# Feed-forward weight sums of an encoder trunk: from GpSimd to VectorE and to accumulating loads

## The chip, the cores and the metric

The kernel runs on one core of a Trainium2 chip. The core has five engines with a queue of instructions each: TensorE (PE: matrix products into PSUM banks), VectorE (DVE), ScalarE (ACT), GpSimd (POOL) and SyncE (SP, which here only issues loads and stores). An engine takes its instructions in order; one that waits for a semaphore holds up all behind it. Sixteen DMA engines move data between device memory and SBUF. The metric is device time of one execution in microseconds, lower is better.

## The reference

The reference is an encoder trunk for 512 tokens of width 1024: two layers, each with a feed-forward, a token mixer, an attention into 256 memory tokens and a second feed-forward. Each ends in a layer norm. All is float32.

```python
def swiglu(x, w_gate, w_up, w_down):
    return (jax.nn.silu(x @ w_gate) * (x @ w_up)) @ w_down
...
    for i in range(DEPTH):
        y = swiglu(x, ffn_w_gate[i, 0], ffn_w_up[i, 0], ffn_w_down[i, 0])
        x = layer_norm(ALPHA * x + 0.5 * y, ln_g[i, 0], ln_b[i, 0])
        ...
        y = swiglu(x, ffn_w_gate[i, 1], ffn_w_up[i, 1], ffn_w_down[i, 1])
        x = layer_norm(ALPHA * x + 0.5 * y, ln_g[i, 3], ln_b[i, 3])
```

The change touches the four calls of `swiglu` alone. Their hidden width is 2816.

## The kernel before

**Precision.** TensorE is fed with the rounded type float32r. To keep float32 accuracy each operand is split: ScalarE copies it rounded (the high part), VectorE subtracts that from the original (the low part). `split` does both, `wide` does it for a block of weights into two new buffers. Each product is then three matmuls (`mm3`): high by high, high by low, low by high.

**Groups.** `ffn` cuts the hidden width into five groups of 512 columns and a rest. Of the first group most is done apart; for the other four the gate and the up projection (1024 x 512 weights each) are multiplied by a 2 x 2 block scheme with seven products in place of eight. Such a projection is called a half-chunk in what follows; it is one call of `quarters`. Its weights are four quarters of 512 x 256: a (upper rows, first columns c1), b (lower rows, c1), c (upper, c2), d (lower, c2). The products, by the scheme's numbers and in the order of the program, need these weights: 1: a; 6: a + c + d; 5: c + d; 2: b; 7: a + c; 4: d; 3: a + b + c + d. The tokens' sums are made once per feed-forward. The way down (512 rows of `w_down`) is done the same way by `down_steps`, with quarters "11", "12", "21", "22" of 256 x 512, and the sums t1 = 12 + 11 (product 5), t2 = t1 + 22 (product 6), t2 + 21 (product 4) and 12 + 22 (product 7).

**Steps.** Each product is a step with three parts: `load` (issues the loads of its weights), `prep` (sums, splits) and `product` (matmuls, and what reads the bank after them). `pipeline` writes the parts in an order in which a step's load stands three steps ahead of its product and its prep two. A group is 14 products of the gate and up half-chunks (24 matmuls of 256 columns each), each paired with one of 14 pieces of the previous group's way down (6 matmuls of 512 columns each).

**Who adds.** `mix(..., aside)` puts a sum on GpSimd where `aside` is true, else on VectorE. On GpSimd are, per half-chunk, v = a + c (into a new buffer) and c = c + d (in place); per way down t1 = 12 + 11 (new buffer) and 12 = 12 + 22 (in place): 32 x 2 + 20 x 2 = 104 sums of 128 x 1024 elements. On VectorE are a = a + c and a = a + b, and t2 = t1 + 22 and t2 = t2 + 21.

**What sets the order.** Nothing runs when the methods are called. `Recorder` stores every instruction as an `Op` with its operands; `Graph.emit` then plans them: it steps through time with an assumed cost per instruction (`Graph.cost`) and an assumed delay until its result can be used, and each engine takes the ready instruction that was recorded first. The order in which the plan starts instructions is the order on the engines' queues. Since all of them are issued from `emit` and `record`, the profile gives nearly all of them one line, L143, and they are told apart by the names of their tiles. Loads by SyncE are assumed to be usable 2000 ns after their issue cost, DMAs issued by GpSimd 4000 ns after 700 ns.

**Buffers.** Weights, sums, split parts and hidden activations all lie in `slab` buffers of 128 x 1024 float32, of which there are 27 (`BUFS`). They are given out in the order of the calls of `slab`; a load waits until the buffer that it is given is free. In PSUM there are three banks "a" (hidden products), two "d" and three "t" (down products and others).

The only accumulating loads before are in `add_x`: GpSimd issues four DMAs of 128 rows of 4 KB that add x onto what stands in SBUF (`accum_op=ALU.add`), in the first feed-forward.

## Time and profile before

| | |
|---|---|
| median of 3 runs | 2236.86 us (2235.01 to 2237.48) |
| profiled execution | 2237.42 us, span 2235.6 us |
| TensorE busy | 2153.6 us (96%), granted clock 0.992 |
| VectorE busy | 1821.6 us (81%) |
| ScalarE busy | 1060.4 us (47%) |
| GpSimd busy | 556.4 us (25%), of it 295.1 us in the 104 weight sums, 2838 ns each on average |
| device memory | 219.27 MB read, 100 GB/s over the span |

The span runs from the first to the last instruction of the profiled execution; the rest of its time lies around it. Busy times are sums over the whole span. Since stages differ, the prediction reads stretches of the span and not these shares. "a<-raw,slab" in a row means: writes a bank "a", reads tiles "raw" and "slab". A product of a hidden group shows as MATMUL into "a", its way down as MATMUL into "d" and "t". In the chain's rows "x24" counts matmuls, and 24 of them make one product. PE's busy time has modelled ends.

### The profile page before, as it was taken

Reading aid. Unit: us, or ns where it says so; the run is one execution under the profiler, and the core shown is the slowest. Engines: PE = TensorE matmul, PEld = TensorE weight load, DVE = VectorE, ACT = ScalarE, POOL = GpSimd, SP = SyncE. Lnnn points to the kernel's source line nnn. Section 1 sums busy time; section 2 is a strip of 40 time slices with the busy share of each in tenths; the row PEclk is TensorE's granted clock in tenths of the full one; section 3 lists DMA queues with packets and bytes.
Section 4 is the critical chain, followed back from the end, with each engine's and each line's share of the span. In section 5 each row is a group of like instructions: output and inputs, shape, how many; then the busy total and the mean of one; then the engine's idle time right before and its main releaser. Section 6 shows DMA issues by size and latency. Waiting matters only on the chain.

```text
span 2235.6 us, 33852 instructions
## 1 busy us (share of the span) xinstructions
PE 2153.6 (96%) x13408; PEld 1924.2 (86%) x13408; DVE 1821.6 (81%) x2429; ACT 1060.4 (47%) x1671; POOL 556.4 (25%) x499
## 2 busy tenths in 40 slices
PE   9999999999999999999999999999999999999997
PEld 7988887778998898888799888888989988988886
DVE  7899998788755869999878999977677558699997
ACT  4554443467443544444534454435554435444442
POOL 2222314544000112232212123314330001122322
PEclk9999999999999999999999999999999999999999
DMA  5432342102432324324323233435554323233241
GB/s 179 136 96 90 109 140 84 38 10 73 133 125 86 112 67 151 95 86 141 95 76 104 86 96 93 156 105 147 154 157 130 115 97 102 67 113 104 87 132 57
DMA packets 182799, 236.15 MB, mean 106 GB/s; under 512 B 9328, under 2 KB 142064, under 8 KB 182640
## 3 DMA queue, kind: packets, MB, share of 16 engines
q1 hardware_dynamic: 178704, 221.14, 32.2%
q0 software_dynamic: 3648, 12.59, 1.9%
q8 instruction: 105, 1.72, 0.3%
q14 instruction: 54, 0.44, 0.1%
q10 hardware_dynamic: 288, 0.26, 0.0%
HBM read 219.27 MB, written 4.19 MB: 100 GB/s over the span
## 4 chain that ended last, share of the span: by engine, by line
PE 67%; DVE 25%; issue 3%; ACT 2%; POOL 1%; DMA 0%; DVEq 0%; SPq 0%; POOLq 0%; ACTq 0%
PE a L143 41%; DVE slab L143 19%; PE d L143 17%; PE t L143 10%; DVE t L143 3%; DVE x L143 2%; ACT slab L143 1%; POOL slab L143 1%; DVE a L143 0%; POOL rms8y L143 0%; ACT t L143 0%; DMA gain<-ab_k_gain 0%; ACT junk L143 0%; POOL lny L143 0%; DMA raw<-x_t 0%
## 5 line engine op out<-in xcount | busy, mean ns | idle before, releaser
L143 DVE TENSOR_TENSOR slab<-slab,slab 128x1024 fp32r<-128x1024 f32 (+3 forms) x582 | 756.3, 1336 | 23.1 <-ACT slab L143 22.3
L143 ACT CAST slab<-slab 128x1024 fp32r<-128x1024 f32 (+2 forms) x478 | 455.5, 984 | 295.3 <-DVE slab L143 150.6
L143 PE MATMUL a<-slab,slab 128*128 128x256 f32 (+3 forms) x2744 | 589.2, 307 | 2.2 <-ACT t L143 1.1
L143 PE MATMUL a<-xh,slab 128*128 128x256 f32 (+2 forms) x2480 | 560.4, 315 | 3.0 <-DVE slab L143 1.9
L143 POOL TENSOR_TENSOR slab<-slab,slab 128x1024 f32<-128x1024 f32 x104 | 295.1, 2838 | 883.2 <-PE t L143 345.8
L143 PEld LDWEIGHTS a<-slab,slab 128*128 128x128 f32 x2744 | 448.0, 191 | 34.2 <-DVE slab L143 5.0
L143 PE MATMUL d<-slab,slab 128*128 128x512 f32 (+2 forms) x1856 | 459.7, 384 | 4.7 <-ACT slab L143 2.9
L143 PEld LDWEIGHTS a<-xh,slab 128*128 128x128 f32 x2480 | 416.8, 191 | 37.4 <-DVE slab L143 2.8
L143 PE MATMUL a<-raw,slab 128*128 128x256 f32 x2048 | 398.2, 287 | 38.7 <-DVE t L143 17.5
L143 PE MATMUL a<-xl,slab 128*128 128x256 f32 (+1 forms) x1240 | 390.5, 315 | 0.0
L143 PEld LDWEIGHTS d<-slab,slab 128*128 128x128 f32 x1856 | 329.7, 190 | 63.9 <-DVE slab L143 4.8
L143 PEld LDWEIGHTS a<-raw,slab 128*128 128x128 f32 x2048 | 331.2, 193 | 59.1 <-DVE slab L143 21.2
L143 PEld LDWEIGHTS a<-xl,slab 128*128 128x128 f32 x1240 | 236.3, 191 | 17.9
L143 PE MATMUL t<-slab,slab 128*128 128x512 f32 (+1 forms) x792 | 195.6, 383 | 1.4 <-DVE x L143 0.7
L143 DVE TENSOR_TENSOR slab<-raw,slab 128x1024 fp32r<-128x1024 f32 (+2 forms) x140 | 172.0, 1248 | 15.8 <-ACT slab L143 15.3
L143 POOL TENSOR_TENSOR t<-t,l 128x256 f32<-128x256 f32 (+2 forms) x104 | 84.6, 835 | 367.9 <-DVE l L143 367.7
L143 PEld LDWEIGHTS t<-slab,slab 128*128 128x128 f32 x792 | 136.6, 189 | 24.1 <-issue 2.4
L143 ACT CAST slab<-t 128x512 fp32r<-128x512 f32 (+2 forms) x205 | 110.1, 563 | 90.0 <-PE t L143 67.5
L143 DVE TENSOR_TENSOR slab<-t,slab 128x512 fp32r<-128x512 f32 (+2 forms) x205 | 126.9, 642 | 17.3 <-ACT slab L143 16.5
L143 ACT CAST slab<-raw 128x1024 fp32r<-128x1024 f32 (+1 forms) x132 | 131.3, 1025 | 18.0 <-DMA raw<-mem_w_kv 7.6
L143 DVE SCALAR_TENSOR_TENSOR x<-d,x 128x512 f32<-128x512 f32 x164 | 111.9, 684 | 34.1 <-PE d L143 33.5
L143 ACT COPY t<-a 128x512 f32<-128x512 f32 x96 | 56.1, 585 | 131.9 <-DVE a L143 97.7
(122 smaller groups left out, 2209.3 us busy)
## 6 DMA issues: line engine op xcount, KB each, us to landing
slab<-ffn_w_gate SPq DMA_DIRECT2D x86, 512.0 KB
slab<-ffn_w_up SPq DMA_DIRECT2D x86, 512.0 KB
slab<-ffn_w_down SPq DMA_DIRECT2D x80, 512.0 KB
slab<-t SPq DMA_DIRECT2D x96, 128.0 KB
raw<-mem_w_kv SPq DMA_DIRECT2D x8, 1024.0 KB
raw<-mem_w_kv SPq DMA_DIRECT2D x16, 512.0 KB
raw<-mem_w_q SPq DMA_DIRECT2D x8, 1024.0 KB
raw<-mem_w_o SPq DMA_DIRECT2D x8, 1024.0 KB
```

The lines of the kernel that those rows point to most:

```text
L143: op.call = lambda: fn(*args, **kw)
```

## The change

No weight sum of the feed-forward is left on GpSimd. In a half-chunk VectorE makes three sums when product 6 is prepared: v = a + c, u = c + d (in c's buffer), a = a + u. After a has been split for product 6, a load adds b onto it from device memory (`plus`), and the result is split again for product 3. b is also loaded plainly, as before, for product 2. In a way down VectorE makes t1 and t2; a load adds "22" onto "12" once t1 is made, and a load adds "21" onto t2 once t2 has been split for product 6. That makes 32 + 40 = 72 accumulating loads of 512 KB, issued by GpSimd, of 512 rows of 1 KB (gate, up) or 256 rows of 2 KB (down). "d" is fetched in the step of product 6 and "12" in that of product 1; the new buffers of v and t1 are taken in `prep` and not in `load`. The planner is told that an accumulating load costs 1200 ns to issue and is usable 9000 ns later.

```diff
@@ class Op, Graph.cost, Graph.record, Graph.emit
-            return max(n * out.ap[0][1] * 4 / 205.0, 600.0) if engine == "sync" else 700.0
+            return max(n * out.ap[0][1] * 4 / 205.0, 600.0) if engine == "sync" else 1200.0 if "accum_op" in kw else 700.0
...
-            end = now[e] + {"sync": 2000.0, "tensor": 160.0}.get(e, 4000.0 if op.dma else 70.0)
+            end = now[e] + {"sync": 2000.0, "tensor": 160.0}.get(e, 9000.0 if op.adds else 4000.0 if op.dma else 70.0)
@@ class Kernel
-    def mix(self, dst, x, y, op, aside=False):
-        (self.nc.gpsimd if aside else self.nc.vector).tensor_tensor(out=dst, in0=x, in1=y, op=op)
+    def plus(self, z, w, q, c):
+        self.nc.gpsimd.dma_start(out=z, in_=w[512 * q : 512 * q + 512, c : c + 256].rearrange("(k p) f -> p k f", p=P), accum_op=ALU.add)
+        return z
+
+    def mix(self, dst, x, y, op):
+        self.nc.vector.tensor_tensor(out=dst, in0=x, in1=y, op=op)
         return dst
@@ quarters
-        places = {1: ("a", 0, c1), 6: ("c", 0, c2), 5: ("d", 1, c2), 2: ("b", 1, c1)}
-
         def load(m):
-            if m in places:
-                name, q, c = places[m]
-                raw[name] = self.quarter(w, q, c)
-            if m == 6:
-                raw["v"] = mix(self.slab(F32, (P, 4, 256)), raw["a"], raw["c"], ALU.add, True)
-            elif m == 5:
-                mix(raw["c"], raw["c"], raw["d"], ALU.add, True)
+            if m == 1:
+                raw["a"] = self.quarter(w, 0, c1)
+            elif m == 6:
+                raw["c"] = self.quarter(w, 0, c2)
+                raw["d"] = self.quarter(w, 1, c2)
+            elif m == 2:
+                raw["b"] = self.quarter(w, 1, c1)
 
         def prep(m):
             if m == 6:
-                mix(raw["a"], raw["a"], raw["c"], ALU.add)
-            elif m == 3:
-                mix(raw["a"], raw["a"], raw["b"], ALU.add)
-            left[m] = self.wide(raw[{1: "a", 6: "a", 5: "c", 2: "b", 7: "v", 4: "d", 3: "a"}[m]])
+                raw["v"] = mix(self.slab(F32, (P, 4, 256)), raw["a"], raw["c"], ALU.add)
+                raw["u"] = mix(raw["c"], raw["c"], raw["d"], ALU.add)
+                mix(raw["a"], raw["a"], raw["u"], ALU.add)
+            left[m] = self.wide(raw[{1: "a", 6: "a", 5: "u", 2: "b", 7: "v", 4: "d", 3: "a"}[m]])
+            if m == 6:
+                self.plus(raw["a"], w, 1, c1)
@@ down_steps
+        def plus(z, name):
+            nc.gpsimd.dma_start(out=z, in_=part(name).rearrange("(b p) f -> p b f", p=P), accum_op=ALU.add)
+
         def load(m):
             if m == 1:
                 fetch("11")
+                fetch("12")
             elif m == 6:
-                fetch("12")
                 fetch("22")
-                raw["t1"] = mix(self.slab(F32, (P, 2, 512)), raw["12"], raw["11"], ALU.add, True)
             elif m == 2:
                 fetch("21")
-                mix(raw["12"], raw["12"], raw["22"], ALU.add, True)
 
         def prep(m):
             if m == 6:
+                raw["t1"] = mix(self.slab(F32, (P, 2, 512)), raw["12"], raw["11"], ALU.add)
                 raw["t2"] = mix(self.slab(F32, (P, 2, 512)), raw["t1"], raw["22"], ALU.add)
+                plus(raw["12"], "22")
...
-            elif m == 2:
-                mix(raw["t2"], raw["t2"], raw["21"], ALU.add)
...
             right[m] = self.wide(raw[{1: "11", 6: "t2", 2: "21", 5: "t1", 3: "22", 7: "12", 4: "t2"}[m]])
+            if m == 6:
+                plus(raw["t2"], "21")
```

**First pair: GpSimd's queue** in the third feed-forward, an up half-chunk, a gate half-chunk, a way down and the next up half-chunk. Before (slab_2212, 2255 and 2303 are "a" of the three half-chunks, slab_2278 is "12"):

```order
L143 TENSOR_TENSOR slab_2216_2297<-slab_2212_2293,slab_2215_2296 128x1024
L143 TENSOR_TENSOR slab_2215_2296<-slab_2215_2296,slab_2225_2306 128x1024
L143 TENSOR_TENSOR slab_2260_2341<-slab_2255_2336,slab_2259_2340 128x1024
L143 TENSOR_TENSOR slab_2259_2340<-slab_2259_2340,slab_2264_2345 128x1024
L143 TENSOR_TENSOR slab_2280_2361<-slab_2278_2359,slab_2261_2342 128x1024
L143 TENSOR_TENSOR slab_2278_2359<-slab_2278_2359,slab_2279_2360 128x1024
L143 TENSOR_TENSOR slab_2307_2388<-slab_2303_2384,slab_2306_2387 128x1024
L143 TENSOR_TENSOR slab_2306_2387<-slab_2306_2387,slab_2316_2397 128x1024
```

Of the changed kernel at the same place (slab_2262 is "12", slab_2285 is t2):

```order
L143 DMA slab_2212_2293<-ffn_w_up 128x4x256
L143 DMA slab_2255_2336<-ffn_w_gate 128x4x256
L143 DMA slab_2262_2343<-ffn_w_down 128x2x512
L143 DMA slab_2285_2366<-ffn_w_down 128x2x512
L143 DMA slab_2303_2384<-ffn_w_up 128x4x256
```

Eight additions have become five issues of accumulating loads, one a half-chunk and two a way down.

**Second pair: VectorE's queue at product 6 of that gate half-chunk.** In it slab_2255 is a, slab_2259 is c; a row that writes x2 or x3 reads a down bank, one that reads "a_" reads a bank of a hidden product. Before:

```order
L143 TENSOR_SCALAR x2_6_87<-d_2251_2332,x2_6_87 128x512
L143 TENSOR_TENSOR slab_2255_2336<-slab_2255_2336,slab_2259_2340 128x1024
L143 TENSOR_SCALAR x3_7_88<-d_2254_2335,x3_7_88 128x512
L143 TENSOR_TENSOR slab_2266_2347<-slab_2255_2336,slab_2265_2346 128x1024
L143 TENSOR_TENSOR slab_2276_2357<-slab_2259_2340,slab_2275_2356 128x1024
```

Of the changed kernel (slab_2265 is v, slab_2260 is d):

```order
L143 TENSOR_TENSOR slab_2265_2346<-slab_2255_2336,slab_2259_2340 128x1024
L143 TENSOR_TENSOR slab_2242_2323<-a_2229_2310,t2_2211_2292 128x512
L143 TENSOR_TENSOR slab_2259_2340<-slab_2259_2340,slab_2260_2341 128x1024
L143 TENSOR_SCALAR x3_7_88<-d_2254_2335,x3_7_88 128x512
L143 TENSOR_TENSOR slab_2255_2336<-slab_2255_2336,slab_2259_2340 128x1024
L143 TENSOR_TENSOR slab_2272_2353<-slab_2261_2342,slab_2271_2352 128x1024
L143 TENSOR_TENSOR t2_2223_2304<-a_2238_2319,t2_2223_2304 128x512
L143 TENSOR_TENSOR slab_2267_2348<-slab_2255_2336,slab_2266_2347 128x1024
```

One sum ahead of the split of product 6 (the row that writes slab_2266, now slab_2267) has become three, with bank reads and another split between them.

**Third pair: VectorE's queue in the first feed-forward's first group, up half-chunk, from the split of product 6 to that of product 3.** Its "a" is slab_107, its "b" slab_125. Before:

```order
L143 TENSOR_TENSOR slab_122_203<-slab_107_188,slab_121_202 128x1024
L143 TENSOR_TENSOR slab_132_213<-t2_129_210,slab_132_213 128x512
L143 TENSOR_TENSOR slab_135_216<-slab_125_206,slab_134_215 128x1024
L143 TENSOR_TENSOR slab_107_188<-slab_107_188,slab_125_206 128x1024
L143 TENSOR_TENSOR a_124_205<-a_124_205,t2_118_199 128x512
L143 TENSOR_TENSOR slab_139_220<-slab_111_192,slab_138_219 128x1024
L143 TENSOR_TENSOR slab_142_223<-slab_82_163,slab_141_222 128x1024
L143 TENSOR_TENSOR slab_143_224<-t2_140_221,slab_143_224 128x512
L143 TENSOR_TENSOR slab_145_226<-slab_120_201,slab_144_225 128x1024
L143 TENSOR_TENSOR slab_148_229<-slab_107_188,slab_147_228 128x1024
```

Of the changed kernel:

```order
L143 TENSOR_TENSOR slab_122_203<-slab_107_188,slab_121_202 128x1024
L143 TENSOR_TENSOR slab_127_208<-slab_110_191,slab_126_207 128x1024
L143 TENSOR_TENSOR slab_131_212<-slab_83_164,slab_130_211 128x1024
L143 TENSOR_TENSOR slab_132_213<-t2_129_210,slab_132_213 128x512
L143 TENSOR_TENSOR slab_135_216<-slab_125_206,slab_134_215 128x1024
L143 TENSOR_TENSOR slab_139_220<-slab_120_201,slab_138_219 128x1024
L143 TENSOR_TENSOR a_124_205<-a_124_205,t2_118_199 128x512
L143 TENSOR_TENSOR slab_142_223<-slab_65_146,slab_141_222 128x1024
L143 TENSOR_TENSOR slab_143_224<-t2_140_221,slab_143_224 128x512
L143 TENSOR_TENSOR slab_145_226<-slab_111_192,slab_144_225 128x1024
L143 TENSOR_TENSOR slab_148_229<-slab_107_188,slab_147_228 128x1024
```

VectorE's own addition of b onto a (the row that writes slab_107) is gone; the accumulating load onto slab_107 has to start after the first of these rows and land before ScalarE's copy for the last one, with nine rows between.

More of the change, by code (lines that the diff above doesn't have):

```diff
@@ L41 @@
 class Op:
-    __slots__ = ("engine", "ns", "call", "deps", "users", "wait", "ready", "end", "frees", "index", "rank", "dma")
+    __slots__ = ("engine", "adds", "ns", "call", "deps", "users", "wait", "ready", "end", "frees", "index", "rank", "dma")
 class Space:
@@ L138, in record @@
         op = Op()
-        op.engine, op.index, op.dma = engine, len(self.ops), method == "dma_start"
+        op.engine, op.index, op.dma, op.adds = engine, len(self.ops), method == "dma_start", "accum_op" in kw
         op.rank = op.index
```

## The prediction

> **What bounds the kernel now.** I read the page first (busy shares, chain), then the chain in order of time, then busy times by stretch, then the instructions by group inside one period of the feed-forward.
>
> ```profile
> span 2235.6 us, 33852 instructions
> PE 2153.6 (96%) x13408; PEld 1924.2 (86%) x13408; DVE 1821.6 (81%) x2429; ACT 1060.4 (47%) x1671; POOL 556.4 (25%) x499
> PE 67%; DVE 25%; issue 3%; ACT 2%; POOL 1%; DMA 0%; DVEq 0%; SPq 0%; POOLq 0%; ACTq 0%
> ```
>
> TensorE is busy nearly throughout, so no change to other engines can win more than the holes in it; but a quarter of the chain is VectorE, and the chain in order of time shows where:
>
> ```profile
> 195.50 7.55 DVE slab L143 x8
> 259.51 7.55 DVE slab L143 x8
> ...
> 944.65 7.55 DVE slab L143 x8
> 1008.67 7.55 DVE slab L143 x8
> ...
> 1174.02 2.87 PE a L143 x24
> 1178.28 2.87 PE a L143 x24
> ...
> 1306.87 7.55 DVE slab L143 x8
> 1370.89 7.55 DVE slab L143 x8
> ...
> 2060.20 7.55 DVE slab L143 x8
> 2124.22 7.55 DVE slab L143 x8
> ```
>
> All four feed-forwards show the same piece of VectorE work, returning after 64.0 us: one of their groups (14 products of a hidden chunk, each followed by one of the 14 products of the chunk before on its way down). Where no engine is late, such a pair takes 1178.28 - 1174.02 = 4.26 us, so a group needs 14 x 4.26 = 59.6 us of TensorE. It takes 64.02 (1370.89 - 1306.87): 4.38 us are lost in each.
>
> ```profile
> 1174.02:1220.86 46.84, 46.84 (x333) 43.99 (x332) 38.79 (x44) 25.79 (x34) 9.63 (x4) 1.00 0.34 103
> 1306.87:1370.89 64.02, 60.90 (x422) 55.84 (x421) 60.17 (x64) 30.21 (x38) 18.52 (x6) 1.00 0.32 99
> sum 790.00, PE 748.61 PEld 688.29 DVE 751.93 ACT 375.79 POOL 216.15; mean PE 187.15 PEld 172.07 DVE 187.98 ACT 93.95 POOL 54.04
> ```
>
> Columns: us, then busy time of PE, weight loads, DVE, ACT, POOL; clock, DMA share, GB/s. First row: the third feed-forward's first group, 11 pairs without a hole, VectorE 38.79 of 46.84 us (83%) busy. Second row: the full period, VectorE 60.17 us busy where TensorE needs 59.6. The sum row adds the four stretches in which the feed-forwards run their groups (107 to 305, 862 to 1056, 1230 to 1420, 1965 to 2173): TensorE idle 790.0 - 748.6 = 41.4 us. The period of the second row shows 64.02 - 60.90 = 3.12 us idle for 4.38 lost (the modelled ends cover the rest), so 41.4 idle stand for 41.4 / 3.12 x 4.38 = 58 us lost, 13 periods' worth. That is the most this change can return.
>
> Why VectorE is late, inside that period (instructions by group, then in order of time on each engine):
>
> ```profile
> L143 DVE TENSOR_TENSOR slab<-slab,slab 128x1024 fp32r<-128x1024 f32 x21 | 31.1, 1516 | 0.6 <-ACT slab L143 0.6
> L143 ACT CAST slab<-slab 128x1024 fp32r<-128x1024 f32 x21 | 21.5, 1048 | 17.8 <-DVE slab L143 12.7 <-PE d L143 4.6 <-PE a L143 0.4
> L143 POOL TENSOR_TENSOR slab<-slab,slab 128x1024 f32<-128x1024 f32 x6 | 18.5, 3087 | 45.5 <-PE t L143 35.6 <-PE d L143 7.1 <-DMA slab<-ffn_w_gate 2.6
> L143 DVE TENSOR_TENSOR slab<-slab,slab 128x1024 f32<-128x1024 f32 x6 | 7.2, 1210 | 0.0
> L143 DVE TENSOR_TENSOR slab<-slab,slab 128x512 fp32r<-128x512 f32 x3 | 3.7, 1219 | 0.0
> L143 DVE TENSOR_TENSOR slab<-t,slab 128x512 fp32r<-128x512 f32 x3 | 2.0, 674 | 0.0
> ...
> 1312.92 7.10 POOL L143 TENSOR_TENSOR slab<-slab,slab 128x1024 f32<-128x1024 f32 x2 [14.60 <-PE t L143]
> 1312.08 2.34 DVE L143 TENSOR_TENSOR slab<-slab,slab 128x1024 fp32r<-128x1024 f32 x2
> 1315.54 5.56 DVE L143 TENSOR_TENSOR slab<-slab,slab 128x1024 fp32r<-128x1024 f32 x2
> ...
> 1341.01 2.66 POOL L143 TENSOR_TENSOR slab<-slab,slab 128x1024 f32<-128x1024 f32 x1 [20.99 <-PE t L143]
> 1341.91 3.43 DVE L143 TENSOR_TENSOR slab<-slab,slab 128x512 fp32r<-128x512 f32 x2
> 1345.27 0.68 DVE L143 TENSOR_TENSOR t<-a,t 128x512 f32<-128x512 f32 x1
> 1346.10 0.36 PE L143 MATMUL a<-raw,slab 128*128 128x256 f32 x1 [0.91 <-DVE t L143]
> ```
>
> Two subtractions of 128x1024 take 2.34 us, and 5.56 us when GpSimd's weight sums run from 1312.92 to 1320.02. The same at 1341.91; there VectorE then reads the product bank at 1345.27, and TensorE, which wanted that bank, starts at 1346.10, late by 0.91. So GpSimd's six sums cost VectorE 21 x (1516 - 1210) = 6.4 us, and 3 x (1219 - 674) = 1.6 us more: 8.0 us of its 60.17.
>
> **The change, part by part.**
>
> *GpSimd's 104 sums go.* GpSimd itself was idle 45.5 us of the period, so its own 18.5 us return nothing; what returns is VectorE's 8.0 us.
>
> *VectorE gets 32 more sums* (three in place of two in each of 32 half-chunks; two for two in the 20 down chunks): 2 a group, at 1.21 us each 2.4 us. VectorE: 60.17 - 8.0 + 2.4 = 54.5 us, against TensorE's 59.6: 91%, and TensorE sets the period. What is left of the 4.38 us is not shown. At 83% nothing was lost (first stretch), at 60.17 / 59.6 = 101% all of 4.38; on the straight line between them 91% loses 2.0 us, and if VectorE only costs where it exceeds TensorE, 0. I take 1.2, since the loss must bend upwards towards 100% but the three sums of product 6 now stand in one burst. Of the 13 periods' worth I count 12 (three a feed-forward), because some holes end on ScalarE or at a stage's start: 12 x (4.38 - 1.2) = 38 us. Ends: 12 x (4.38 - 2.0) = 29, and all 58.
>
> *72 accumulating loads come*, issued by GpSimd: "a" becomes product 3's weights by adding "b", "12" product 7's, "t2" product 4's, each after VectorE and ScalarE have split what it held. None exists there now; the nearest rows are the loads that add x onto sums in the first feed-forward (view of DMA issues, GpSimd in order of time, and the queues between 92 and 122 us; the last row is the queue in the period above):
>
> ```profile
> x<-x POOLq DMA_DIRECT2D x4, 512.0 KB, 7.5
> ...
> 94.59 1.06 POOL L143 DMA_DIRECT2D x<-x  x1 [15.20 <-ACT x L143]
> 112.92 0.82 POOL L143 DMA_DIRECT2D x<-x  x1 [0.54 <-ACT x L143]
> ...
> q1 hardware_dynamic: 3216, 3.92, 40.7%
> q0 software_dynamic: 576, 2.10, 38.0%
> ...
> q1 hardware_dynamic: 5305, 6.29, 32.0%
> ```
>
> Same bytes, same adding: 7.5 us from issue to landing, 0.82 to 1.06 us of it on GpSimd, in a stretch where the 16 DMA engines were 40.7 + 38.0 = 79% taken. That is the lower end. These moved 128 rows of 4 KB; the new ones move 512 rows of 1 KB or 256 of 2 KB. If GpSimd's part grows with the rows, 4 x 0.82 = 3.3 us, it is 10.0: the upper end. I take 8.3, nearer the row that is alike in all but the row length.
>
> The up half-chunk gives the least time. In the first feed-forward's first group 9 VectorE rows stand between the split of product 6 and that of product 3 (front, third pair of lists), 6 of 1024 columns and 3 of 512. Back to back a long one takes 2.34 - 1.21 = 1.13 us, a short one 0.67 at most: 8.8 us. ScalarE's copy, 1.05, must come before the split, which leaves the load 7.7. In the other 15 groups 12 or 13 rows stand there, 6 long and 6 or 7 short: 10.8 or 11.5 us, 9.7 at least for the load. At 8.3 it is hidden in 15 groups and 0.6 us late in one, whose VectorE has 17% to spare: nothing. At 10.0 it costs up to 15 x 0.3 + 2.3 = 7 us. The gate half-chunk has about 14 us, the down sums 22 or more (12 in each feed-forward's last chunk). Behind a late load stand ScalarE's and VectorE's whole queues; behind GpSimd's wait to issue one stand only further such loads, x's four, and in the last chunk the two layer-norm loads and the sums into x.
>
> DMA: 2.10 MB took 38.0% of 16 engines x 30 us, 87 us per MB; six loads a group, 3.1 MB, are 274 us of 16 x 59.6: 29% beside 32%. 61% is under the 79% in which x was loaded; I cost it at nothing, the cover being the lead of the weights, next.
>
> *Loads move.* "d" is fetched one step earlier (product 6 needed a + c + d before too), "12" together with "11", and the buffers of v and t1 are taken two steps later.
>
> ```profile
> SPq L143 <- DVE slab L143: 22.1, 3, 12.4
> SPq L143 <- PE a L143: 20.2, 5, 7.8
> SPq L143 <- PE t L143: 15.1, 2, 14.2
> ...
> 1346.29 2.65 POOL L143 TENSOR_TENSOR slab<-slab,slab 128x1024 f32<-128x1024 f32 x1 [2.62 <-DMA slab<-ffn_w_gate]
> 1355.50 1.21 DVE L143 TENSOR_TENSOR slab<-slab,slab 128x1024 f32<-128x1024 f32 x1
> ```
>
> The load queue waits for free buffers for 57 of 64 us, so an earlier place in it asks no more of memory. GpSimd's c + d started when d landed, 1346.29; VectorE's first use of that sum, for product 6, is at 1355.50. Nine microseconds of lead cover the move; if they shrank to nothing, ScalarE's copy for product 6 would be late next.
>
> **Sum.** The profiled execution took 2237.42 us (span 2235.6, 1.8 around it), 0.6 above the median of the runs, 2236.86. 2237.4 - 38 = 2199. Its own range: 2237 - 58 = 2179, and 2237 - 29 + 7 = 2215.
>
> **Rivals.**
>
> *The adding loads land late* (slower). For: they are the only new wait at the head of two queues, and their length with short rows is unmeasured. Against: 7.5 us in a busier stretch. Each microsecond beyond 9.7 costs up to one in each of 16 up half-chunks, so the 38 us are gone at 9.7 + 38 / 16 = 12.1, from where this decides; at 13, 3.3 x 16 = 53 us are lost, 2199 + 53 = 2252.
>
> *GpSimd cannot issue beside VectorE.* If the issue had to wait out two of VectorE's long rows, 2.3 us, a load would take 8.3 + 2.3 = 10.6, late by 0.9 us in 15 groups and 2.9 in one: 16 us, 2215. Against: x's 0.82 to 1.06 us. [...]
>
> *The burst keeps VectorE late.* Three sums and a split in a row, 3 x 1.21 + 1.21 = 4.8 us, exceed the 4.26 us of a pair, and a bank read behind them is late as at 1345.27. For: holes follow single delays of 2 to 3 us now. Against: the new order puts bank reads between the sums (front, second pair). If 3.4 of 4.38 us stay: 12 x 1.0 = 12, 2225.
>
> *It returns nothing*: the slow subtractions coincide with GpSimd's sums but the holes come from the written order, which would then be as full of them. Against: the bank read at 1345.27, late right behind such a pair. 2237.
>
> **How the numbers follow.** The forecast 0.60, the burst 0.12, the blocked issue 0.04, nothing returned 0.06, late loads 0.18. Likeliest: 2199. From 2180 to 2240 leaves out the late loads past break-even, up to 0.18, and little else. A measurement of this kernel tells 0.2% (4.5 us) from no change: faster is the forecast, the burst and the blocked issue, 0.76; same is nothing returned, 0.06; slower the late loads, 0.18.
>
> **What would show it.** Right: the 128x1024 subtractions at 1.21 us mean in the feed-forward; the period at 60 to 61.5 us; VectorE near 54 us in it; TensorE's waits on VectorE's t and slab a third of now. The loads: ScalarE or VectorE waiting on a weight DMA in the up half-chunk would show them late, with the issue-to-landing median of the adding loads above 9.7. Wrong: a period of 64 us with short subtractions (order), or a longer one whose chain runs through the adding loads.

## The result and the profile after

The changed kernel takes 2180.27 us (median of 4 executions, 2179.13 to 2181.91) against 2237.17 us (2235.01 to 2238.43) for the kernel before, run beside it: 57 us less, ratio 0.9747, 95% interval 0.973 to 0.9764. The forecast was 2199 us in a range of 2180 to 2240: the sign is right, and the time lies at the range's lower edge, 0.27 us inside it with two of the four executions below it, 19 us below the forecast.

The page of the profile after (span, busy shares, chain by engine):

```profile
span 2179.3 us, 33960 instructions
PE 2135.5 (98%) x13408; PEld 1923.0 (88%) x13408; DVE 1726.6 (79%) x2461; ACT 1066.8 (49%) x1671; POOL 350.6 (16%) x467
PE 91%; DVE 3%; DMA 2%; ACT 1%; POOL 1%; issue 1%; SPq 1%; DVEq 0%; POOLq 0%; ACTq 0%
```

VectorE has dropped from 25% of the chain to 3%. The chain in order of time (start, duration, what) no longer passes through it in the feed-forwards:

```profile
119.46 10.72 DMA slab<-ffn_w_up
174.75 5.75 PE a L143 x48
234.37 5.75 PE a L143 x48
...
852.25 10.79 DMA slab<-ffn_w_down
909.49 5.75 PE a L143 x48
969.11 5.75 PE a L143 x48
...
1259.02 5.75 PE a L143 x48
1318.64 5.75 PE a L143 x48
...
1996.84 5.75 PE a L143 x48
2056.46 5.75 PE a L143 x48
```

The pieces that return are TensorE's own, and they return after 59.62 us in all four feed-forwards: TensorE's pace, with nothing lost. What is new are two loads of feed-forward weights in the chain. Now one whole period by stretch (columns as in the prediction), and instructions by group inside it:

```profile
1259.02:1318.64 59.62, 59.62 (x422) 56.05 (x422) 55.06 (x66) 30.32 (x38) 4.95 (x5) 1.00 0.57 142
```

```profile
L143 DVE TENSOR_TENSOR slab<-slab,slab 128x1024 fp32r<-128x1024 f32 x21 | 25.0, 1218 | 0.3 <-ACT slab L143 0.3
L143 DVE TENSOR_TENSOR slab<-slab,slab 128x1024 f32<-128x1024 f32 x8 | 9.7, 1218 | 0.0
L143 DVE TENSOR_TENSOR slab<-slab,slab 128x512 fp32r<-128x512 f32 x3 | 2.0, 682 | 0.0
```

The subtractions take 1218 ns where they took 1516, the short ones 682 where they took 1219; VectorE makes 8 sums in place of 6 and is busy 55.06 us, 92% of the period. TensorE's waits on VectorE, of before (first two rows) and of after:

```profile
PE a L143 <- DVE t L143: 17.5, 17, 1.2
PE a L143 <- DVE slab L143: 16.9, 27, 4.4
```

```profile
PE a L143 <- DVE t L143: 4.0, 1, 4.0
PE a L143 <- DVE slab L143: 0.8, 4, 0.3
```

The one wait of 4.0 us that is left stands in the first feed-forward, at 133.31, behind the first of the two DMAs in the chain.

The accumulating loads in the view of DMA issues (last number: median us from issue to landing), GpSimd's part of them, and the queues from 92 to 130 us, where x's four loads run beside the first group:

```profile
slab<-ffn_w_down POOLq DMA_DIRECT2D x40, 512.0 KB, 6.0
slab<-ffn_w_gate POOLq DMA_DIRECT2D x16, 512.0 KB, 6.0
slab<-ffn_w_up POOLq DMA_DIRECT2D x16, 512.0 KB, 5.9
x<-x POOLq DMA_DIRECT2D x4, 512.0 KB, 9.7
...
L143 POOL DMA_DIRECT2D slab<-ffn_w_down x40 | 47.8, 1194 | 306.7 <-DVE slab L143 273.7 <-issue 20.7 <-PE a L143 12.3
L143 POOL DMA_DIRECT2D slab<-ffn_w_up x16 | 20.5, 1282 | 321.8 <-PE a L143 149.4 <-DVE slab L143 140.7 <-issue 31.8
...
q0 software_dynamic: 1648, 3.67, 55.5%
q1 hardware_dynamic: 3985, 4.94, 40.8%
```

The new loads land after 6 us, sooner than x's did before; x's own have become slower (9.7 where it was 7.5), in a stretch whose DMA engines are 96% taken, and the two new loads of `ffn_w_down` in that stretch take 12.6.

### The profile page after: what moved, and what is told of

Its sections match the earlier page's. It is cut to its first block, busy times and chain, and to the rows that moved or that the text cites. A ratio compares the mean times of both kernels' runs of the same rounds, so it can differ in the third digit from the quotient of the medians.

```text
span 2179.3 us, 33960 instructions
## 1 busy us (share of the span) xinstructions
PE 2135.5 (98%) x13408; PEld 1923.0 (88%) x13408; DVE 1726.6 (79%) x2461; ACT 1066.8 (49%) x1671; POOL 350.6 (16%) x467
## 4 chain that ended last, share of the span: by engine, by line
PE 91%; DVE 3%; DMA 2%; ACT 1%; POOL 1%; issue 1%; SPq 1%; DVEq 0%; POOLq 0%; ACTq 0%
PE a L143 56%; PE d L143 21%; PE t L143 13%; DVE slab L143 2%; DVE x L143 1%; DVE t L143 1%; ACT slab L143 1%; POOL slab L143 1%; SPq L143 1%; DMA slab<-ffn_w_down 0%; DMA slab<-ffn_w_up 0%; DMA raw<-ab_w_out 0%; ACT t L143 0%; DMA gain<-ab_k_gain 0%; ACT junk L143 0%
## 5 line engine op out<-in xcount | busy, mean ns | idle before, releaser
L143 DVE TENSOR_TENSOR slab<-slab,slab 128x1024 fp32r<-128x1024 f32 (+3 forms) x614 | 696.9, 1163 | 50.0 <-ACT slab L143 27.2
L143 PE MATMUL d<-slab,slab 128*128 128x512 f32 (+2 forms) x1856 | 453.4, 383 | 4.2 <-ACT slab L143 2.9
L143 PE MATMUL a<-raw,slab 128*128 128x256 f32 x2048 | 390.2, 283 | 4.0 <-DVE t L143 4.0
L143 POOL DMA_DIRECT2D slab<-ffn_w_down x40 | 47.8, 1194 | 306.7 <-DVE slab L143 273.7
```

The source lines that it names most:

```text
L143: op.call = lambda: fn(*args, **kw)
```

## The experiments

Two questions were open. First, why nothing at all is lost at 92%: is it VectorE's amount of work that makes TensorE wait (the prediction's straight line from 83% to 101%), or the way GpSimd's sums hold up single operations of VectorE? Second, what the accumulating loads are worth and cost. Every kernel below was run with the kernel before beside it; ratios are to that one, with 95% intervals.

**All sums on VectorE.** No accumulating load of weights is left; a + b, t2 + 21 and 12 + 22 become VectorE's, four more sums a group than in the changed kernel.

```diff
@@ quarters, prep
+            elif m == 3:
+                mix(raw["a"], raw["a"], raw["b"], ALU.add)
-            if m == 6:
-                self.plus(raw["a"], w, 1, c1)
@@ down_steps, prep
-                plus(raw["12"], "22")
+            elif m == 2:
+                mix(raw["t2"], raw["t2"], raw["21"], ALU.add)
             elif m == 7:
+                mix(raw["12"], raw["12"], raw["22"], ALU.add)
-            if m == 6:
-                plus(raw["t2"], "21")
```

> The changed kernel with its 72 accumulating loads taken out and those sums made by VectorE where the kernel before needs them (a + b ahead of product 3, 12 + 22 ahead of product 7, t2 + 21 ahead of product 4); nothing on GpSimd. VectorE gets 4 more sums a group: 55.1 + 4 x 1.13 = 59.6 us, as long as TensorE's 59.6. Theory (VectorE's time against TensorE's decides): some holes come back, 1 to 4 us a group, 12 groups: 2192 to 2229, I say 2205, with 128x1024 subtractions still at 1.22 us. Rival (only the overlap with GpSimd mattered, VectorE's load does not): 2180, period 59.6.

Measured 2173.12 us (2171.95 to 2174.28), ratio 0.9719 (0.9705 to 0.9734): 7 us faster than the changed kernel. One period:

```profile
1250.82:1310.43 59.61, 59.61 (x423) 56.04 (x422) 59.08 (x68) 30.35 (x39) 1.65 (x3) 1.00 0.37 111
```

VectorE is busy 59.08 of 59.61 us, 99%, and TensorE still never stops in the period. So the straight line is wrong: in this order VectorE's amount costs nothing up to 99% of TensorE's time. And the accumulating loads are not what brings the gain: of the 9.1 us between the two profiled executions, compared matmul by matmul, 5.8 lie before 168 us, around the changed kernel's hole at 129, and 1.8 around the second feed-forward's start.

**The loads alone.** The sums that are wanted at once (v, c + d, t1) go back to GpSimd; the late ones stay loads.

```diff
-                raw["v"] = mix(self.slab(F32, (P, 4, 256)), raw["a"], raw["c"], ALU.add)
-                raw["u"] = mix(raw["c"], raw["c"], raw["d"], ALU.add)
+                raw["v"] = mix(self.slab(F32, (P, 4, 256)), raw["a"], raw["c"], ALU.add, True)
+                raw["u"] = mix(raw["c"], raw["c"], raw["d"], ALU.add, True)
@@ down_steps
-                raw["t1"] = mix(self.slab(F32, (P, 2, 512)), raw["12"], raw["11"], ALU.add)
+                raw["t1"] = mix(self.slab(F32, (P, 2, 512)), raw["12"], raw["11"], ALU.add, True)
```

> The other half alone: late sums by accumulating loads, but v, c + d and t1 on GpSimd as before (5 sums a group). VectorE keeps 3 sums a group and loses 5/6 of 8.0 us to overlap: 55.1 - 5 x 1.13 + 6.7 = 56.1 us, 94% of TensorE's time. Theory: between no loss (at 92% the changed kernel lost none) and 1.5 us a group: 2180 to 2200, subtractions at about 1.45 us mean. Rival (GpSimd's sums on product 6's way make holes by themselves, whatever VectorE's load): 2215 or more.

Measured 2218.45 us (2215.36 to 2225.99), ratio 0.9927 (0.9907 to 0.9947): a third of the gain, in the rival's range. A period by stretch, and a hole in the first feed-forward (time, duration, engine, operation; in brackets what it waited for):

```profile
1285.36:1346.80 61.44, 60.08 (x423) 55.88 (x422) 56.06 (x60) 30.33 (x39) 19.41 (x10) 1.00 0.56 137
```

```profile
223.07 2.39 POOL L143 TENSOR_TENSOR slab<-slab,slab 128x1024 f32<-128x1024 f32 x1 [11.97 <-PE t L143]
223.84 5.48 DVE L143 TENSOR_TENSOR slab<-slab,slab 128x512 fp32r<-128x512 f32 x2
225.85 2.39 POOL L143 TENSOR_TENSOR slab<-slab,slab 128x1024 f32<-128x1024 f32 x1 [0.39 <-DMA slab<-ffn_w_gate]
229.25 0.68 DVE L143 TENSOR_TENSOR t<-a,t 128x512 f32<-128x512 f32 x1
230.07 0.36 PE L143 MATMUL a<-raw,slab 128*128 128x256 f32 x1 [2.62 <-DVE t L143]
...
L143 DVE TENSOR_TENSOR slab<-slab,slab 128x1024 fp32r<-128x1024 f32 x1 | 3.4, 3395 | 0.0
L143 DVE TENSOR_TENSOR slab<-slab,slab 128x512 fp32r<-128x512 f32 x1 | 2.2, 2164 | 0.0
```

VectorE is busy 56.06 us, three less than with all sums on it, and yet 1.8 us of the period are lost; the periods of this kernel differ, from 60.43 to 65.98 us in its chain. In the hole, the row of two subtractions bears the shape of the first alone: the last two rows, which keep shapes apart, show that it holds a short one and a long one. By the rows above they take 682 and 1218 ns; here they take 2164 and 3395 ns, while two sums of GpSimd run beside them. The bank read behind them is late, and TensorE waits 2.62 us for it.

**Idle work on GpSimd, reading or writing.** To the changed kernel two operations without a use are added, each on a buffer whose last reader has just passed (b in a half-chunk, 21 in a way down): two subtractions, which read SBUF, in the one kernel; five memsets, which only write it, in the other. The planner is given 2.16 ns per element for such a subtraction, in both kernels.

```diff
             left[m] = self.wide(raw[{1: "a", 6: "a", 5: "u", 2: "b", 7: "v", 4: "d", 3: "a"}[m]])
+            elif m == 2:
+                for _ in range(2): nc.gpsimd.tensor_tensor(out=raw["b"], in0=raw["b"], in1=raw["b"], op=ALU.subtract)
@@ and in the other kernel
+                for _ in range(5): nc.gpsimd.memset(raw["b"], 0.0)
```

> The changed kernel plus idle work on GpSimd: two subtractions of 128x1024 on the buffer of b and of 21 after its last use, 6 a group, whose results nobody reads. Theory (GpSimd reading SBUF holds up VectorE): VectorE loses about 8 us a group, 55.1 + 8.0 = 63 us against 59.6, period 64 to 66: 2235 to 2255, subtractions near 1.5 us mean. Rival (the written order made the holes, not the overlap): 2180 to 2190.

> Control for the run before: the same buffers held and GpSimd busy as long at the same places, by five memsets in place of two subtractions, so it reads nothing. Theory (reading is what collides): 2180 to 2187, subtractions at 1.22 us. Rival (any GpSimd work on SBUF, or the longer hold of the buffers, makes the holes): as the run before, 2235 or more.

Reading: 2218.43 us (2216.51 to 2220.52), ratio 0.9922 (0.9907 to 0.9937). Writing: 2172.66 us (2171.2 to 2175.04), ratio 0.9715 (0.9699 to 0.9731). The groups of GpSimd's idle work and of VectorE's subtractions, and one period, of the reading kernel and then of the writing one:

```profile
L143 POOL TENSOR_TENSOR slab<-slab 128x1024 f32<-128x1024 f32 x104 | 262.0, 2519 | 194.4 <-DVE slab L143 180.7 <-DMA slab<-ffn_w_up 8.6 <-PE t L143 2.3
L143 DVE TENSOR_TENSOR slab<-slab,slab 128x1024 fp32r<-128x1024 f32 x408 | 553.2, 1375 | 45.2 <-ACT slab L143 19.5 <-PE a L143 18.0 <-POOL slab L143 7.1
...
1279.88:1342.06 62.18, 60.10 (x422) 55.89 (x421) 61.28 (x66) 30.35 (x38) 19.88 (x10) 1.00 0.53 136
```

```profile
L143 POOL MEMSET slab<- 128x1024 f32 x264 | 260.3, 986 | 204.0 <-DVE slab L143 174.0 <-issue 8.5 <-DMA slab<-ffn_w_up 8.1
L143 DVE TENSOR_TENSOR slab<-slab,slab 128x1024 fp32r<-128x1024 f32 x408 | 491.9, 1226 | 41.1 <-PE a L143 18.3 <-ACT slab L143 18.0 <-POOL slab L143 3.9
...
1253.43:1313.05 59.62, 59.62 (x422) 56.05 (x422) 55.04 (x66) 30.33 (x38) 19.24 (x20) 1.00 0.58 142
```

GpSimd is busy the same 260 us in both. Between the two lie 46 us (the reading kernel is 38 above the changed one), and writing costs nothing. So GpSimd's time is free here, and what hurts is that it reads SBUF beside VectorE's subtractions (1375 against 1226 ns mean). The reading kernel stayed below the 2235 us that were expected at least: VectorE was stretched by 6.2 us in the period (61.28 - 55.06) and not by 8. The writing kernel came out 8 us below the changed one, which was not forecast: its first feed-forward has no hole although the DMAs are as crowded (98% from 92 to 130 us); the load that was late there landed after 9.5 us in place of 10.7. Compared matmul by matmul, 5.3 of the 6.0 us between the two profiled executions lie before 168 us, at this place. The planner had other work to place, so the order is not quite the same; why the load is sooner stays open.

**Half the reading.** One idle subtraction each time in place of two.

```diff
-                for _ in range(2): nc.gpsimd.tensor_tensor(out=raw["b"], in0=raw["b"], in1=raw["b"], op=ALU.subtract)
+                nc.gpsimd.tensor_tensor(out=raw["b"], in0=raw["b"], in1=raw["b"], op=ALU.subtract)
```

> As the kernel with GpSimd's two idle subtractions on b and on 21, but one of them each time: half the reading. It should stretch VectorE's work by about half of 6.2 us, to 58.2 us of 59.6, below the 59.1 that cost nothing where all sums were on VectorE; and nothing waits for these subtractions. Theory of single stretched operations ahead of bank reads: holes stay though VectorE is below TensorE, 2190 to 2212 us. Rival, that only VectorE's total beyond TensorE's costs: no holes, 2171 to 2184 us.

Measured 2192.7 us (2189.85 to 2194.33), ratio 0.9802 (0.9788 to 0.9817).

```profile
1266.60:1327.56 60.96, 59.85 (x422) 55.98 (x421) 56.90 (x65) 30.22 (x38) 13.63 (x7) 1.00 0.55 139
...
1283.24 1.78 DVE L143 TENSOR_TENSOR t<-t,slab 128x512 f32<-128x512 f32 x1
```

VectorE was stretched by 1.8 us (56.90 - 55.06), less than expected, and TensorE loses 1.3 us in this period, with VectorE 2.2 us below the 59.08 that cost nothing. It is the place of the delay that costs, not the sum: one operation takes 1.78 us in place of some 0.68 beside a GpSimd subtraction, and TensorE then waits 1.11 us at 1285.26 for the bank read two operations behind it. One point of the expectation was wrong: ScalarE does wait for these subtractions (3.1 us in the period, for the buffer to come free). VectorE had no idle time ahead of that bank read.

**The old order without the reading.** The kernel before, with each of GpSimd's weight sums left out and three memsets of about its length in all put in its place.

```diff
-        (self.nc.gpsimd if aside else self.nc.vector).tensor_tensor(out=dst, in0=x, in1=y, op=op)
+        if aside:
+            for _ in range(3):
+                self.nc.gpsimd.memset(dst, 0.5)
+        else:
+            self.nc.vector.tensor_tensor(out=dst, in0=x, in1=y, op=op)
```

> The kernel before, with each of GpSimd's 104 weight sums replaced by three memsets of the same destination (three times some 1.0 us, about as long as the sum's 2.84 us; planned as long as the sum was). The sums themselves are left out, so four of the seven products of a half-chunk and three of a way down are of other numbers. Order, buffers, plain loads and planned costs are those of before; GpSimd writes SBUF as long as before but reads nothing. Theory of the held-up reads: the order of before was good, and all it lost came from VectorE's operations being stretched while GpSimd reads: subtractions 1.22 us mean, 2172 to 2185 us. Rival, the written order (the last rival of the prediction) or VectorE waiting for GpSimd's results: the holes stay, 2205 us or more.

Measured 2173.41 us (2171.73 to 2173.61), ratio 0.9713 (0.9697 to 0.9729).

```profile
1252.07:1311.68 59.61, 59.61 (x422) 56.03 (x422) 53.10 (x63) 30.23 (x39) 16.89 (x19) 1.00 0.35 107
```

The order of before holds TensorE's pace once GpSimd no longer reads for these sums: 62 us come back, more than the change gave. The prediction's last rival (the holes come from the written order) is out.

**A delay of VectorE's own.** Is it only the length of a delay that the plan does not know of? In the first kernel the planner is told that a float32 sum of 1024 columns costs 100 ns; in the second VectorE also writes v twice in a row.

```diff
+            if method == "tensor_tensor" and n == 1024 and not wide and out.tensor.dtype == F32:
+                return 100.0
@@ quarters, second kernel only
                 raw["v"] = mix(self.slab(F32, (P, 4, 256)), raw["a"], raw["c"], ALU.add)
+                mix(raw["v"], raw["a"], raw["c"], ALU.add)
```

> The changed kernel, but the planner is told that a float32 sum of 128x1024 elements on VectorE costs 100 ns in place of 1139; nothing runs on GpSimd that did not before. So 8 sums a group, 1.22 us each on the chip, come as some 9 us a group that the plan does not know of, about as much as GpSimd's overlap added in the kernel before (8.0), while VectorE's work stays at some 55 us of 59.6. Theory that delays cost because the plan does not know them (single lumps of 1 to 4 us in front of bank reads): holes return, 2200 to 2237 us. Rival, that something else in the overlap with GpSimd does it, or that VectorE's slack takes up what the plan does not know: 2178 to 2185 us.

> The kernel with the hidden cost, and in each half-chunk VectorE writes v = a + c twice in a row (the same numbers again). A delay of four sums, some 4.6 us, now stands unknown to the plan ahead of product 6, and VectorE's work is some 57.5 us of 59.6, still below the 59.1 of the kernel with all sums on VectorE. Theory that a delay costs once it is as long as the two to three microseconds that GpSimd's reads put in front of a bank read: holes in every group, 0.5 us or more each, 2196 to 2215 us. Rival, that VectorE's own work, in whatever lumps, is taken up as long as it stays below TensorE's: at most 2192 us.

The hidden cost alone: 2188.44 us (2186.9 to 2190.17), ratio 0.9783 (0.9768 to 0.9797). With v written twice: 2203.41 us (2200.85 to 2206.9), ratio 0.9848 (0.9831 to 0.9864). A period of the first; then a period of the second, and the end of a hole in it:

```profile
1264.54:1324.17 59.63, 59.63 (x422) 55.95 (x422) 55.25 (x65) 30.22 (x39) 4.95 (x4) 1.00 0.58 142
```

```profile
1275.97:1336.86 60.89, 60.08 (x422) 55.89 (x422) 57.45 (x67) 30.23 (x39) 4.95 (x4) 1.00 0.57 139
...
1322.39 3.61 DVE L145 TENSOR_TENSOR slab<-slab,slab 128x1024 fp32r<-128x1024 f32 x3
1325.91 0.68 DVE L145 TENSOR_TENSOR t<-a,t 128x512 f32<-128x512 f32 x1
1326.75 0.36 PE L145 MATMUL a<-raw,slab 128*128 128x256 f32 x1 [0.75 <-DVE t L145]
```

Some eight microseconds a group that the plan does not know of (8 x (1.14 - 0.1); 1.14 us is what the planner otherwise takes for such a sum) are taken up in the period shown, and the periods in the chain are 59.62 to 59.89 us. The time lies between the two ranges of the expectation, 8 us behind the changed kernel. By TensorE's waits in the two traces, 3.90 against 1.48 us at the second feed-forward's start, 1.38 us in each of two stages outside the feed-forwards, and 1.14, 0.44 and 1.02 us in the last groups of three feed-forwards add 7.8 us, and the hole at 130 us is 2.2 us shorter. So this half of the theory fell: not every unknown delay costs.

One more sum in the same place, and TensorE loses 1.1 to 1.8 us in each period of the chain behind the one with the late load (3.5 us there, 111.74 to 174.87), with no GpSimd work in it but issues, and VectorE's total (57.45) below the 59.08 that cost nothing. At the hole shown the bank read stands behind a subtraction and two sums that the plan counts at 100 ns each. So the delay need not come from GpSimd. Of the sums that the plan counts at 100 ns, the order here seems to take up three in a row, about 3.1 us more than planned (3 x (1.14 - 0.1)), and not four, 4.2; both are estimates, and no run shows the delay itself.

**Late loads.** The accumulating load onto "a" in four DMAs of 128 KB, or in eight of 64 KB, each planned at a share of the issue cost; and, apart from that, the planner's old figures for such loads.

```diff
+        src = w[512 * q : 512 * q + 512, c : c + 256].rearrange("(k p) f -> p k f", p=P)
+        for k in range(4):
+            self.nc.gpsimd.dma_start(out=z[:, k], in_=src[:, k], accum_op=ALU.add)
@@ and in the kernel with eight, inside that loop
+            for f in range(2):
+                part = slice(128 * f, 128 * f + 128)
+                self.nc.gpsimd.dma_start(out=z[:, k, part], in_=src[:, k, part], accum_op=ALU.add)
@@ the kernel with the old figures: Graph.cost and Graph.emit
-1200.0 if "accum_op" in kw else 700.0
+700.0
-9000.0 if op.adds else 4000.0 if op.dma else 70.0
+4000.0 if op.dma else 70.0
```

> Each accumulating load onto a cut into 4 DMAs of 128 rows, planned as one, so the order of all other engines stays. Four issues of 0.82 us or more in place of one of 1.28: landing 2 to 2.5 us later, about 8.2 us after the first issue. Theory (free until 9.7): 2180, within 3 us. Rival (it lands just in time now): 16 x 2 = 32 us more, 2212.

> The same in 8 DMAs of 128 rows of 512 bytes. Eight issues of 0.82 us or more: 5 to 6 us later, landing 11 to 12 us after the first issue, 1.6 us or more past 9.7. Theory (each microsecond past 9.7 costs up to 16): 2190 to 2220, I say 2206, with ScalarE waiting for the weight loads of the up half-chunk. Rival (VectorE's spare time absorbs it): 2180 to 2186.

> The changed kernel planned with the costs of before for the adding loads (700 ns to issue, usable 4000 ns later; measured: 1.2 to 1.3 and 4.8 us). The splits that need them stand up to 5 us earlier in the queues. Theory: they wait about 1.3 us each at the queue's head, which VectorE's 4.5 us a group spare mostly cover: 2180 to 2195. Rival (the assumed 10.2 us keep the queues free of waits and are needed): 2200 or more.

Four pieces: 2183.41 us (2181.88 to 2184.26), ratio 0.9758 (0.9743 to 0.9772). Eight: 2183.92 us (2183.77 to 2185.49), ratio 0.9762 (0.9748 to 0.9777). Old figures: 2180.62 us (2178.49 to 2185.18), ratio 0.975 (0.9732 to 0.9767). The eight pieces' issues on GpSimd and their landings:

```profile
slab<-ffn_w_gate POOLq DMA_DIRECT2D x128, 64.0 KB, 5.1
slab<-ffn_w_up POOLq DMA_DIRECT2D x128, 64.0 KB, 3.9
...
L143 POOL DMA_DIRECT2D slab<-ffn_w_up x128 | 113.5, 2045 | 309.7 <-issue 263.2 <-DVE slab L143 46.5
```

These are medians of single pieces. Read issue by issue in the trace, it takes 10.3 us in the up half-chunks (median; 8.8 to 12.2) from the first piece's issue to the last one's landing. That is past the prediction's 9.7 us in nine of the 16, and in four of them ScalarE stands idle for it, 1.2 to 1.8 us each; the run is 3.7 us behind the changed kernel. With four pieces the last lands after 6.5 us (median), 1.4 us or more ahead of ScalarE's copy, and that run is 3.1 behind all the same (3 were expected at most), so the lateness itself costs next to nothing. With the old figures the copies stand earlier: in eleven of the 16 up half-chunks ScalarE's copy starts 0.3 to 0.7 us after the landing, where the changed kernel leaves 2.3 to 4.8, and the time is that of the changed kernel within 0.4 us. So the 9 us that the planner assumes are not needed. Loads that are later still were not tried.

**x in four parts.** `add_x` issues its four loads one a group in place of all after the first group, to thin out the crowded stretch.

```diff
-            if i == 0:
-                for t in range(NT):
-                    self.add_x(t)
@@ ffn, in the loop over groups
+            if i == 0:
+                steps.append(only(lambda t=g - 1: self.add_x(t)))
```

> The changed kernel with the four loads that add x issued one a group in place of all in the first feed-forward's first group. There the chain now runs 10.7 us through a weight load and TensorE loses 4.1 us at 129 us. Theory (those loads and the new ones crowd the DMA engines there): the hole goes, 2176. Rival (the load is late for its buffer, not for the DMA engines): 2180.

Measured 2177.54 us (2176.32 to 2177.68), ratio 0.9731 (0.9717 to 0.9746). From 92 to 130 us, and the load that was late:

```profile
q1 hardware_dynamic: 4360, 5.30, 46.4%
q0 software_dynamic: 1216, 2.10, 33.5%
...
121.23 8.41 DMA slab<-ffn_w_up
```

The DMA engines are 80% taken in place of 96%, the plain load of `ffn_w_up` that TensorE waits for lands after 8.4 us in place of 10.7, and 2.7 us come back: the crowding made that hole, of which 1.7 of 4.0 us are left.

## Why the prediction was right, and where it was off

**What bounds it.** The steady groups gave back 4.40 us each (64.02 to 59.62), as the 4.38 of the prediction says. That 57 us came in all, just under the cap of 58, is in part a coincidence: with all sums on VectorE, and with memsets in the old order, the time is 63.6 and 62.4 us below the kernel before, so the cap was some 5 us low, and the loads took about 7 of what there was. That the time still lies inside the stated range, by 0.27 us, is luck too (the sum's own range began at 2179).

**GpSimd's sums cost VectorE 8.0 us a group.** Right, by the subtractions' means (1218, 682). One of its rows is read too simply: the two subtractions of 3.43 us at 1341.91 are a short one and a long one, and only the short one is held up, 2.30 us in place of 0.68. That it is the reading that does it is shown by the pair of idle kernels: VectorE's long subtractions took 1375 ns mean with GpSimd's idle subtractions and 1226 with its memsets; the prediction could not tell reading from running. The long subtraction of the hole above (3395 ns) started while a GpSimd sum ran, one that ended at 228.24 (225.85 + 2.39), and itself ended 1.1 us after that, at 229.32 (223.84 + 5.48).

**VectorE at 54.5 us.** 55.06 measured, 0.6 over; that the 29 long sums and subtractions take 1218 ns and not 1210 makes 0.2 of it.

**What is left of the 4.38 us.** This is the step that failed. Taken were 1.2 us a group, between a straight line (2.0) and nothing; nothing was the end that came, and 12 x 1.2 = 14.4 of the 19 us by which the forecast was off lie here. Another 4.4 lie in counting 12 periods of the 13. The line had two points, 83% and 101%, and took VectorE's share for the cause at both. The runs put this in its place: at 99% of planned work nothing is lost, at 94 to 96% in which single operations came late, 1.3 to 1.8 us in the periods shown. These side by side, from the rows above (the last column is argued from the edits, its microseconds are the estimates above):

| kernel | VectorE busy, us | period, us | delays unknown to the plan |
|---|---|---|---|
| before | 60.17 | 64.02 | GpSimd's six sums |
| after | 55.06 | 59.62 | none |
| all sums on VectorE | 59.08 | 59.61 | none |
| hidden cost | 55.25 | 59.63 | three sums, 3.1 us |
| hidden cost, v twice | 57.45 | 60.89 | four sums, 4.2 us |
| the loads alone | 56.06 | 61.44 | GpSimd's five sums |
| half the reading | 56.90 | 60.96 | GpSimd's three subtractions |
| reading | 61.28 | 62.18 | GpSimd's six subtractions |
| old order, memsets | 53.10 | 59.61 | none |

In the reading kernel and the one before, VectorE's total also exceeds TensorE's 59.6, so there both causes add; how much is due to each was not separated.

**Issue to landing 8.3 us, between 7.5 and 10.0.** It is 6.0, below the lower end. The lower end was x's, and x ran in the more crowded stretch (79% against 57%). GpSimd's part grows little with the rows: 1.19 us for 256 rows and 1.28 for 512, where 128 rows took 0.82 to 1.06 in the kernel before (1.16 on average in the changed one), so the 3.3 us of the upper end were far off. Since 8.3 was priced at nothing, this moved no microsecond.

**DMA at 61%, and the moved loads, both at nothing.** The share is 57% in the period, and there it costs nothing. That it comes near 61% is two errors that cancel. The prediction counts six accumulating loads a group; there are four, one in each of two half-chunks and two in the way down. The queues in the period after (packets, MB, share):

```profile
q1 hardware_dynamic: 5312, 6.29, 33.4%
q0 software_dynamic: 1600, 2.10, 23.3%
```

So 2.10 MB took 23.3% of 16 x 59.62 us, 106 us per MB, where x's took 87. The share does cost something at the two crowded places: the plain loads at 119.46 and 852.25 are in the chain for 10.7 and 10.8 us. The first costs TensorE 4.0 us; spreading x brought 2.7 us back. The prediction compared 61% with the 79% under x's loads, but not the two together: x's loads and two way-down loads fall into the same 38 us, 96%. By the kernel with all sums on VectorE, the loads lose 7 us against sums that cost nothing.

**The rivals.** *Late loads:* TensorE does not wait on one of the new loads in a steady group, and the price, up to a microsecond in each of 16 up half-chunks for each past 9.7, looks too high: loads in eight pieces, past it in nine half-chunks and by 11.6 us taken together, cost 0.5 us more than those in four. The 9.7 itself is of the right size: in the changed kernel's trace ScalarE's copy starts 10.0 us after the issue in the up half-chunks (median; 8.4 to 10.6), about 4 us after the landing. Lateness past 12.1 us, the break-even, was produced in one half-chunk alone (12.2). *Blocked issue:* 1.19 to 1.31 us on GpSimd beside a VectorE that is busy 92%, not 0.8 + 2.3. *The burst:* no hole, since the three sums are planned; in the kernel with four unknown sums it is real, but costs 1.1 to 1.8 us a group, not the 3.4 that the rival took. *Nothing returned:* excluded by the old order with memsets.

**What would show it.** Subtractions (1218 for 1210 ns) and VectorE's waits (a quarter of 17.5, a twentieth of 16.9; "a third" was asked) came as said; the period was expected at 60 to 61.5 and is 59.62.

## What to carry to other kernels

An engine with an in-order queue that is planned well could be filled to 99% here beside the one that sets the pace, so a share of busy time near 100% is by itself no reason to move work away from it; what cost here was a delay of some microseconds that the plan does not know, ahead of an operation that the pacing engine waits for (with v written twice, 1.1 to 1.8 us in each period). Work moved to GpSimd "for free" was such a delay where it read SBUF beside VectorE's operations with both inputs in SBUF: the subtractions of 128x1024 among them took 1428 ns mean over the kernel before and 1230 over the changed one, the rows that add a down bank to x 684 and 687. So price it by what it adds to VectorE's rows beside it, and try giving it back to VectorE before inventing another way, since here plain VectorE sums (2173.1 us) beat the accumulating loads (2180.3). When two sets of transfers are each cheap, add their shares in the one stretch where both run (96% here, where a plain load took 10.7 us and TensorE lost 4.0).

## What the runs showed of the hardware that was not expected

- GpSimd memsets of 128x1024 (986 ns each, 260 us in all) leave VectorE's subtractions at 1226 ns mean; the same time spent in subtractions that read SBUF raises them to 1375 ns.
- The hold-up reaches single operations: a subtraction of 128x512 took 2.16 us in place of 0.68, and the one of 128x1024 behind it 3.40 in place of 1.22, beside two GpSimd sums of 2.39 us. GpSimd's operations take longer at times as well: two of its sums took 7.10 us together in the kernel before, where another took 2.66.
- An accumulating load of 512 KB lands 6.0 us after its issue in the feed-forward, and 9.7 us (x) or 12.6 us (way down) after it where the DMA engines are 96% taken; its issue on GpSimd takes 1.19 us with 256 rows and 1.28 to 1.31 with 512, and a piece of 64 KB 0.89 us (113.5 / 128).
